# One exponential per head with both exponents as its bias, in the decay step of a bidirectional DeltaNet encoder

## The chip, the cores and the metric

The kernel runs on one core of one Trainium2 chip. The metric is the device time of one execution in microseconds (us), lower being better. The engines are TensorE (PE in the rows; its weight loads are PEld), VectorE (DVE), ScalarE (ACT), GpSimd (POOL) and SyncE (SP), whose queue issues all DMAs. Each engine works through its own list of instructions in a fixed order and waits there on semaphores.

## The reference

One encoder layer for two sequences, 4096 and 2048 rows of 1024, cut into 48 tiles of 128 rows. A combined projection feeds three groups of heads: windowed attention, attention to 256 memory rows, and a gated DeltaNet that runs over the sequence in both directions. The groups are gated, concatenated, projected and normalized. The change lies in the DeltaNet, in the decays:

```python
g = jnp.cumsum(g, axis=-1)
causal = jnp.tril(jnp.ones((C, C), bool))
decay = jnp.exp(jnp.where(causal, g[..., :, None] - g[..., None, :], -jnp.inf))
k_beta = k * beta[..., None]
a = jnp.einsum('...id,...jd->...ij', k_beta, k) * decay
...
qk = jnp.einsum('...id,...jd->...ij', q, k) * decay
```

The kernel holds these matrices transposed, the index j in the partitions. It puts the factor beta (and a constant scale, 2 to the power -20) into the same exponent. For one tile, direction and head an entry is exp(g_i + mask - g_j + ln beta_j - 20 ln 2), where g_i lies along the free axis and the last terms are one number per partition. The kernel takes chunks of 128 rows, one tile, instead of 64.

## The kernel before, in words

A first phase (lines 1503 to 1526) goes over 24 pairs of tiles: layer norm, projections, a short convolution and windowed attention; its results go to HBM. At its end stand `gates` for the first 8 tiles, the first call of `dn_front`, and the first gate projections (lines 1613 to 1616). A second phase (`pipe`, line 1724) goes over the 24 pairs twice, forwards and then backwards, as the DeltaNet runs. Beside the recurrence the forward pass does the gate projections and the memory attention (`gate_mem`, line 1686), the backward pass the output projection and the last layer norm (`finish`, line 1767).

What one tile and direction of the DeltaNet needs:

- `gates` (line 1362), once for 8 tiles, 6 calls in all: from the raw projections it computes ln beta (tile `lnb`, line 1387) and, by small matmuls into the PSUM tile `psg`, the cumulated g. ACT copies the transposed sums to `cT`, which goes to HBM as `crow`, and copies -g_j from PSUM to `ncum` (line 1410). A DVE instruction then adds LN20 and `lnb` into `psg` in place (line 1411), and ACT takes the exponential of all of it into `egs`.
- `dn_front` (line 1459), for two pairs together: it loads rows of `crow` into the tile `cr` (4 heads of 128x128 for one tile, called `e` in `dn_prep`) and calls `dn_prep`.
- `dn_prep` (line 869), 96 calls: DVE adds the mask to `cr` (line 882); ACT adds `ncum`, one instruction per head (line 884); ACT takes the exponential with `lnb` as bias, one per head (line 886). PE makes the products `psk`, and DVE multiplies them by `cr` into `n` and `p` (lines 898 and 899).
- `dn_invert` (line 933): `n` goes through HBM into `na`, POOL works 60 short instructions on `nb` and `tb`, and the result comes back as `uc`.
- `dn_level` and `dn_chain` (lines 983 and 1035): the recurrence over tiles. Each tile is a series of small matmuls (`psr`, `psx`, `psb`, `psx2`, `pss`); after each, ACT writes the rounded half of a result (`rx`, `shl`) and DVE the rest. DVE's `sf<-pss` ends a tile's link of the series.

The order of every engine's list comes from a planner (class `Plan`, line 56). It records all operations of a phase with a cost for each (`full_cost`, line 137) and schedules them by rank and by free buffers. Seven times it takes new ranks from how late each operation may be, and of the seven orders it keeps the one with the shortest planned span (`order`, line 268). An operation that goes or changes its engine can therefore move any other of its phase. All operations are issued at line 505, so the rows of the profile show that line, and are told apart by tile names.

```python
for h in range(4):
    S.activation(e[:, h], e[:, h], AF.Identity, bias=nc_[:, h:h + 1])
for h in range(4):
    S.activation(e[:, h], e[:, h], AF.Exp, bias=lb[:, h:h + 1])
```

Of the kernel before, what the change touches and what calls it, by code (L numbers as in the profile page):

```python
# [13 lines left out]
AF = mybir.ActivationFunctionType  # L14
ALU = mybir.AluOpType
# [535 lines left out]
def encoder(ctx: ExitStack, tc: tile.TileContext, A, outs):  # L551
    nc = tc.nc
    plan = Plan(tc)
    V, S, G, T, Q = plan.engines()
# [12 lines left out]
    def ctile(shape, dt, name):  # L567
        return const.tile(shape, dt, name=name, tag=name)
# [219 lines left out]
    ncum = ctile([P, 2, NT, 4], F32, "ncum")  # L788
    lnb = ctile([P, 2, NT, 4], F32, "lnb")
# [18 lines left out]
    def split(eng_hi, dst_h, dst_l, src, scale=None):  # L808

        if scale is None:  # L810
            S.activation(dst_h, src, AF.Copy)
            V.tensor_tensor(dst_l, src, dst_h, op=ALU.subtract)
        else:
            S.activation(dst_h, src, AF.Copy, scale=scale)
            V.scalar_tensor_tensor(dst_l, src, scale, dst_h, op0=ALU.mult, op1=ALU.subtract)
# [53 lines left out]
    def dn_prep(pool, psp, dr, t, e, n):  # L869

        fm = pool.tile([P, 8, P], F16, tag="fm", name="fm", bufs=2)
        Q.dma_start_transpose(out=fm, in_=dst_d[t].rearrange("p h t s d -> p (h t s d)"))

        ks = pool.tile([P, 4, P], F16, tag="ks", name="ks", bufs=KSB)
        kv = fm.rearrange("p (h t) m -> p h t m", t=2)[:, :, 1]
        for i in range(2):
            S.activation(ks[64 - 64 * i:128 - 64 * i], kv[64 * i:64 * i + 64], AF.Copy)
        lb = lnb[:, dr, t]
        nc_ = ncum[:, dr, t]
        d = {}  # L880

        V.tensor_tensor(e, e, dmask[dr][2].unsqueeze(1).to_broadcast([P, 4, P]), op=ALU.add)
        for h in range(4):
            S.activation(e[:, h], e[:, h], AF.Identity, bias=nc_[:, h:h + 1])
        for h in range(4):
            S.activation(e[:, h], e[:, h], AF.Exp, bias=lb[:, h:h + 1])
        d["eg"] = egs[:, :, dr, t]

        p = pool.tile([P, 4, P], F32, tag="p", name="p", bufs=1)
        for hp in range(2):  # L890
            hs = slice(2 * hp, 2 * hp + 2)
            psk = psp.tile([P, 2, 2, P], F32, tag="fr", name="psk", bufs=1)
            for h2 in range(2):
                h = 2 * hp + h2
                T.matmul(psk[:, :, h2], lhsT=fm[:, 2 * h + 1, :], rhs=fm[:, 2 * h:2 * h + 2, :],
                         start=True, stop=False)
                T.matmul(psk[:, :, h2], lhsT=ks[:, h, :], rhs=fm[:, 2 * h:2 * h + 2, :], start=False, stop=True)
            V.tensor_tensor(n[:, hs], psk[:, 1], e[:, hs], op=ALU.mult)
            V.scalar_tensor_tensor(p[:, hs], psk[:, 0], -(2.0 ** 10), e[:, hs], op0=ALU.mult, op1=ALU.mult)
        d["n"] = n  # L900
        phl = pool.tile([P, 2, 4, P], F16, tag="phl", name="phl", bufs=2 * PAIRS)
        split(None, phl[:, 0], phl[:, 1], p)
        d["phl"] = phl
        d["t"], d["dr"] = t, dr
        return d
# [247 lines left out]
    bias = biasp.tile([P, AH, 386], F32, name="bias", tag="bias")  # L1153
# [208 lines left out]
    def gates(b, pool, tags):  # L1362

        ts = slice(b * NG, min(NT, b * NG + NG))
        n = ts.stop - ts.start
        xe = pool.tile([P, 2, NG, 16], F32, tag=tags[0][0], name="gx", bufs=tags[0][1])
        w = pool.tile([P, 6, NG, 16], F32, tag=tags[1][0], name="gw", bufs=tags[1][1])[:, :, 0:n]
        x, e = xe[:, 0, 0:n], xe[:, 1, 0:n]
        Q.dma_start(out=x, in_=ab_d[b])
        z = w[:, 0]  # L1370
        V.tensor_tensor(z[:, :, 0:8], x[:, :, 0:8], dtb.unsqueeze(1).to_broadcast([P, n, 8]), op=ALU.add)
        V.tensor_scalar(z[:, :, 8:16], x[:, :, 8:16], -1.0, None, op0=ALU.mult)

        V.tensor_scalar(w[:, 1], z, -1.0, None, op0=ALU.mult)
        V.tensor_tensor(e, z, w[:, 1], op=ALU.min)
        S.activation(e, e, AF.Exp)
        V.tensor_scalar(w[:, 2], e, 2.0, None, op0=ALU.add)
        V.reciprocal(w[:, 2], w[:, 2])
        V.tensor_tensor(w[:, 3], e, w[:, 2], op=ALU.mult)
        V.tensor_tensor(w[:, 4], w[:, 3], w[:, 3], op=ALU.mult)  # L1380
        V.tensor_scalar(w[:, 5], w[:, 4], 1.0 / 15.0, None, op0=ALU.mult)
        for k in range(6, 0, -1):
            V.scalar_tensor_tensor(w[:, 5], w[:, 5], 1.0 / (2 * k + 1), w[:, 4], op0=ALU.add, op1=ALU.mult)
        V.scalar_tensor_tensor(w[:, 5], w[:, 5], 1.0, w[:, 3], op0=ALU.add, op1=ALU.mult)
        V.tensor_scalar(z, z, 0.0, None, op0=ALU.max)
        V.scalar_tensor_tensor(z, w[:, 5], 2.0, z, op0=ALU.mult, op1=ALU.add)
        V.tensor_scalar(lnb[:, :, ts], z[:, :, 8:16].rearrange("p t (d h) -> p d t h", d=2), -1.0, -LN20,
                        op0=ALU.mult, op1=ALU.add)
        g = z[:, :, 0:8]
        V.tensor_tensor(g, g, nea.unsqueeze(1).to_broadcast([P, n, 8]), op=ALU.mult)  # L1390
        V.tensor_scalar(g, g, GMIN, None, op0=ALU.max)
        gg = xe[:, 1].rearrange("p t c -> p (t c)").bitcast(F16)[:, 0:16 * n]
        gg = gg.rearrange("p (a d t h) -> p a d t h", a=2, d=2, h=4)
        gd = g.rearrange("p t (d h) -> p d t h", d=2)
        V.tensor_copy(gg[:, 0], gd)
        V.tensor_tensor(gg[:, 1], gd, gg[:, 0], op=ALU.subtract)
        ps = pj.tile([P, 512], F32, tag="pw", name="psg", bufs=1)
        ps3 = ps[:, 0:24 * n].rearrange("p (i d t h) -> p i d t h", i=3, d=2, h=4)
        pst = ps[0:4 * n, 256:512].rearrange("p (d i) -> p d i", d=2)
        for dr in range(2):  # L1400
            U, L, _ = dmask[dr]
            for i, st in enumerate((U, L, ones16)):
                for a in range(2):
                    T.matmul(ps3[:, i, dr], lhsT=st, rhs=gg[:, a, dr], start=(a == 0), stop=(a == 1))
            for a in range(2):
                T.matmul(pst[:, dr], lhsT=gg[:, a, dr], rhs=U, start=(a == 0), stop=(a == 1))
        cT = pool.tile([P, 2, P], F32, tag=tags[2][0], name="cT", bufs=tags[2][1])[0:4 * n]
        S.activation(cT, pst, AF.Copy)
        Q.dma_start(out=crow_d[b].rearrange("d t h i -> (t h) d i"), in_=cT)
        S.activation(ncum[:, :, ts], ps3[:, 0], AF.Copy, scale=-1.0)  # L1410
        V.scalar_tensor_tensor(ps3[:, 1], ps3[:, 1], LN20, lnb[:, :, ts], op0=ALU.add, op1=ALU.add)
        S.activation(egs[:, :, :, ts], ps3, AF.Exp)

# [45 lines left out]
    def dn_front(pools, psp, dr, pairs, step=2):  # L1459

        H = 4 // len(pairs)
        ds, ns = [], []
        for pool, tiles in zip(pools, pairs):
            t0 = min(tiles)
            rows = []
            for t in range(t0, t0 + 2, step):
                cr = pool.tile([P, step, 4, P], F32, tag="cr", name="cr", bufs=2)
                Q.dma_start(out=cr.rearrange("p t h i -> p (t h i)"),
                            in_=crow_d[t // NG][dr, t % NG:t % NG + step].rearrange("t h i -> (t h i)").partition_broadcast(P))
                rows += [cr[:, i] for i in range(step)]  # L1470
            n = pool.tile([P, 2, 4, P], F32, tag="n", name="n", bufs=PAIRS)
            ns.append(n)
            ds.append([dn_prep(pool, psp, dr, t, rows[t - t0], n[:, i]) for i, t in enumerate(tiles)])
        for pool, ucs, two in zip(pools, dn_invert(pools, dr, ns, H), ds):
            for i, d in enumerate(two):
                d["uc"] = ucs[:, 4 * i:4 * i + 4]
        return ds
# [356 lines left out]
```

## Time and profile before

| what | value |
|---|---|
| median of 3 runs (lowest to highest) | 3352.14 us (3349.26 to 3354.52) |
| profiled execution | 3363.07 us |
| its span, first to last instruction | 3361.0 us |
| busy: PE, DVE, ACT, POOL | 2870.1, 2920.9, 2441.2, 1711.0 us |
| mean granted TensorE clock, share of full | 0.944 |

Busy time is the time in which an engine executes at least one of its instructions. The profile names for each idle stretch the event that ended it, and follows one chain of work back from the last instruction: at each step to what released it, or to the instruction ahead of it on its engine. The chain adds up to the span. Matmuls are pipelined, so a busy PE isn't at its peak.

### The profile page before, as it was taken

To read this page: it belongs to the slowest core of one execution; us is meant where nothing else is said; L and a number is where in the kernel's file an instruction comes from. 1 tells how busy PE (TensorE), PEld (TensorE's weight loads), DVE (VectorE), ACT (ScalarE), POOL (GpSimd) and SP (SyncE) were. 2 spreads that over 40 slices of the span, in tenths; PEclk is the share of its full clock that TensorE was granted. 3 is DMA by queue.
4 is the path that set the end of the run, shared out by engine and by line. 5 is a ranking of instruction groups with operands and counts; after the bars stand their busy time and mean duration, and the time that the engine had idled before them with its cause. 6 is when DMAs were issued, how large, how long until landed. Compare 5 with 4: busy or idle time off the path is not lost.

```text
span 3361.0 us, 82755 instructions
## 1 busy us (share of the span) xinstructions
PE 2870.1 (85%) x29856; PEld 1893.3 (56%) x29856; DVE 2920.9 (87%) x6850; ACT 2441.2 (73%) x6253; POOL 1711.0 (51%) x2611
## 2 busy tenths in 40 slices
PE   5788888788898887767899999999988988998988
PEld 4566666666676665444556555555554544444544
DVE  7999868799999989678889888888878988888997
ACT  4577656767777776688888878777877777777764
POOL 3644424344444334546645455455528666657662
PEclk9899998899999998878999999999998999999999
DMA  6999999999999999898678887778788777877775
GB/s 203 239 224 220 219 222 222 234 230 220 212 233 220 200 224 247 210 223 180 165 191 194 206 181 178 172 161 181 172 190 194 191 183 179 193 179 188 183 175 154
DMA packets 1336916, 671.43 MB, mean 200 GB/s; under 512 B 1127728, under 2 KB 1243312, under 8 KB 1332280
## 3 DMA queue, kind: packets, MB, share of 16 engines
q1 hardware_dynamic: 1336504, 666.14, 86.3%
q8 instruction: 234, 3.83, 0.5%
q14 instruction: 178, 1.46, 0.1%
HBM read 240.12 MB, written 181.49 MB: 125 GB/s over the span
## 4 chain that ended last, share of the span: by engine, by line
DVE 31%; PE 20%; POOL 15%; DMA 13%; issue 10%; ACT 8%; SPq 3%; POOLq 0%; ACTq 0%; DVEq 0%
POOL nb L505 5%; DVE acc L505 5%; POOL tb L505 5%; PE pso L505 5%; PE psg L505 5%; PE psf L505 3%; SPq L505 3%; DVE lg L505 3%; DVE aphl L505 3%; PE psk L505 2%; ACT lg L505 1%; PE psq L505 1%; DMA uc<-ud 1%; PE pslg L505 1%; DVE rx L505 1%
## 5 line engine op out<-in xcount | busy, mean ns | idle before, releaser
L505 PEld LDWEIGHTS <-xT 128*128 128x128 f16 x5760 | 535.5, 99 | 385.2 <-issue 52.5
L505 PE MATMUL psg<-w2a,xT 128*128 128x512 f16 (+1 forms) x2304 | 446.0, 334 | 9.6 <-DVE qtm L505 8.0
L505 PE MATMUL psf<-xT,w1f 128*128 128x256 f16 (+1 forms) x3600 | 439.9, 276 | 14.7 <-DMA xT<-xhl 6.3
L505 PEld LDWEIGHTS <-w1f 128*128 128x128 f16 x3600 | 341.7, 101 | 59.4 <-issue 10.8
L505 POOL TENSOR_TENSOR nb<-nb,tb 128x30 f32<-128x30 f32 (+6 forms) x750 | 348.6, 465 | 49.3
L505 POOL TENSOR_TENSOR tb<-nb,na 128x30 f32<-128x30 f32 (+6 forms) x750 | 342.6, 457 | 48.3
L505 ACT ACTIVATE lg<-lg,mx,scal 128x385 f32<-128x385 f32 (+1 forms) x384 | 263.8, 688 | 122.3 <-DVE mx L505 107.6
L505 PE MATMUL pslg<-kfm,qfm 128*128 128x128 f16 x2240 | 201.0, 233 | 164.1 <-DVE mx L505 149.4
L505 DVE SCALAR_TENSOR_TENSOR acc<-cb,cw,acc 128x256 f32<-128x256 f32 x576 | 329.8, 605 | 4.1 <-POOL cb L505 1.7
L505 PEld LDWEIGHTS <-qfm 128*128 128x128 f16 x2624 | 204.2, 104 | 222.3 <-issue 188.0
L505 PEld LDWEIGHTS <-yT 128*128 128x128 f16 x2304 | 200.1, 99 | 216.1 <-issue 27.7
L505 PE MATMUL pso<-w2a,yT 128*128 128x512 f16 x1152 | 311.4, 394 | 9.6 <-DMA yT<-yhl 7.1
L505 PE MATMUL pso<-w2b,yT 128*128 128x512 f16 x1152 | 298.9, 383 | 0.0
L505 PE MATMUL psg<-w2b,xT 128*128 128x512 f16 x1152 | 289.3, 382 | 3.8 <-DMA w2b<-w_d 3.8
L505 PE MATMUL psq<-w1t,xT 128*128 128x512 f16 x1152 | 287.0, 385 | 0.2 <-ACT cb L505 0.2
L505 DVE TENSOR_TENSOR aphl<-lg,aphl 128x768 f16<-128x768 f32 (+1 forms) x192 | 209.9, 1096 | 49.7 <-ACT aphl L505 49.3
L505 POOL TENSOR_TENSOR n<-raw 128x256 f32<-128x256 f16 x96 | 82.3, 867 | 262.2 <-DMA raw<-cfh 62.1
L505 DVE CUSTOM_DVE_ANT_0 lg<-pslg,bias 128x385 f32<-128x385 f32 (+1 forms) x384 | 195.3, 539 | 17.7 <-PE pslg L505 13.5
L505 POOL TENSOR_TENSOR x<-x,grow 128x1024 f32<-128x1024 f32 x52 | 128.0, 2462 | 121.8 <-ACT x L505 117.6
L505 PEld LDWEIGHTS <-th 64*64 64x64 f16 x2304 | 99.1, 111 | 131.1 <-issue 106.1
L505 PE MATMUL psk<-w1t,xT 128*128 128x272 f16 x1152 | 161.4, 287 | 13.5 <-DVE qktm L505 10.0
L505 PE MATMUL psx<-rx,th 64*64 64x64 f16 x2304 | 126.8, 197 | 41.3 <-DVE rx L505 29.8
(1026 smaller groups left out, 7607.8 us busy)
## 6 DMA issues: line engine op xcount, KB each, us to landing
x<-x SPq DMA_DIRECT2D x48, 512.0 KB, 4.3
xT<-xT SPq DMA_DIRECT2D x24, 1024.0 KB, 5.5
xT<-xT SPq DMA_DIRECT2D x48, 512.0 KB, 4.5
n<-dn SPq DMA_DIRECT2D x96, 256.0 KB, 3.3
r<-x SPq DMA_DIRECT2D x48, 512.0 KB, 4.4
out_dram<-r SPq DMA_DIRECT2D x48, 512.0 KB, 3.8
cr<-crow SPq DMA_DIRECT2D x47, 512.0 KB, 5.1
yhl<-yhl SPq DMA_DIRECT2D x48, 384.0 KB, 3.4
```

The costliest lines, as they stand in the source:

```text
L505: getattr(self.eng[o["e"]], o["name"])(*o["args"], **o["kw"])
```

## The change

The two bias terms are added once per 8 tiles, and one exponential per head takes the sum as its bias. `ncum` now holds -g_j + ln beta_j - 20 ln 2; it is written by DVE instead of ACT, still from `psg`, before `psg` is changed in place.

```diff
@@ dn_prep
-        lb = lnb[:, dr, t]
         nc_ = ncum[:, dr, t]
...
         for h in range(4):
-            S.activation(e[:, h], e[:, h], AF.Identity, bias=nc_[:, h:h + 1])
-        for h in range(4):
-            S.activation(e[:, h], e[:, h], AF.Exp, bias=lb[:, h:h + 1])
+            S.activation(e[:, h], e[:, h], AF.Exp, bias=nc_[:, h:h + 1])
@@ gates
-        S.activation(ncum[:, :, ts], ps3[:, 0], AF.Copy, scale=-1.0)
+        V.scalar_tensor_tensor(ncum[:, :, ts], ps3[:, 0], -1.0, lnb[:, :, ts], op0=ALU.mult, op1=ALU.add)
         V.scalar_tensor_tensor(ps3[:, 1], ps3[:, 1], LN20, lnb[:, :, ts], op0=ALU.add, op1=ALU.add)
```

The planner makes new orders from it for all engines. Three places show what moves. The first is ACT at the first call of `dn_front`, near the end of the first phase (`cr` is the decay tile; `lg`, `aphl` belong to the attention, `cfh` and `acc` to the convolution). Before:

```order
L505 ACTIVATE lg,mx<-lg,mx,scal 128x385 x4
L505 ACTIVATE cr<-cr,ncum 128x128 x2
L505 ACTIVATE cr<-cr,lnb 128x128 x2
L505 ACTIVATE cr<-cr,ncum 128x128 x2
L505 ACTIVATE cr<-cr,lnb 128x128 x2
L505 ACTIVATE cfh<-acc 128x512
L505 ACTIVATE cr<-cr,ncum 128x128
L505 ACTIVATE aphl<-lg 128x768
L505 ACTIVATE cr<-cr,ncum 128x128
L505 ACTIVATE cr<-cr,lnb 128x128 x2
```

Now:

```order
L505 ACTIVATE lg,mx<-lg,mx,scal 128x385 x4
L505 ACTIVATE cr<-cr,ncum 128x128 x7
L505 ACTIVATE cfh<-acc 128x512
L505 ACTIVATE cr<-cr,ncum 128x128
L505 ACTIVATE aphl<-lg 128x768
```

The additions are gone, and the exponentials of two tiles, now named with `ncum`, stand nearly in one piece. In all, ACT's list has 384 instructions `cr<-cr,ncum` and 384 `cr<-cr,lnb` before, and 384 and none now; the 6 copies to `ncum` are gone from it too.

The second is DVE in the first call of `gates` (`gx` is the input of the matmuls into `psg`, `qktm` belongs to the attention). Before:

```order
L505 TENSOR_TENSOR gx<-gw,gx 128x64
L505 SCALAR_TENSOR_TENSOR qktm<-psk_2841,qktm 128x128 x2
L505 SCALAR_TENSOR_TENSOR qktm<-psq,qktm 128x8x64
L505 SCALAR_TENSOR_TENSOR psg<-psg,lnb 128x64
L505 ISA lg,mx<-pslg_590,bias 128x385
```

Now:

```order
L505 TENSOR_TENSOR gx<-gw,gx 128x64
L505 SCALAR_TENSOR_TENSOR qktm<-psk_2841,qktm 128x128 x2
L505 SCALAR_TENSOR_TENSOR qktm<-psq,qktm 128x8x64
L505 SCALAR_TENSOR_TENSOR ncum<-psg,lnb 128x2x32
L505 SCALAR_TENSOR_TENSOR psg<-psg,lnb 128x64
L505 ISA lg,mx<-pslg_590,bias 128x385
```

The new instruction stands right ahead of the one that it must precede.

The third is DVE early in the forward pass, from the end of the recurrence's second tile, `sf<-pss`, to `rx`, with which the third tile goes on (`gate`, `qtm` and `mmx` belong to the gate projections and the memory attention). Before:

```order
L505 SCALAR_TENSOR_TENSOR sf<-pss,st__21316 128x256
L505 TENSOR_TENSOR b_21232<-n,b_21230 64x4x32
L505 TENSOR_TENSOR kc<-kc_21355,kc 128x512
L505 TENSOR_TENSOR shl<-sf,shl 128x256
L505 SCALAR_TENSOR_TENSOR v_21343<-psr,v_21343 128x256
L505 TENSOR_TENSOR phl<-p,phl 128x512
L505 SCALAR_TENSOR_TENSOR rx<-v_21343,rx 128x256
```

Now, with `rx` next after the last row:

```order
L505 SCALAR_TENSOR_TENSOR sf<-pss,st__21308 128x256
L505 TENSOR_TENSOR yhl<-gate,yhl 128x256
L505 TENSOR_TENSOR b_21224<-n,b_21222 64x4x32
L505 SCALAR_TENSOR_TENSOR p<-psk,cr 128x256
L505 TENSOR_TENSOR shl<-sf,shl 128x256
L505 SCALAR_TENSOR_TENSOR qtm<-psg_21516,qtm 128x4x64
L505 TENSOR_REDUCE mmx<-psml 128x2 x2
L505 TENSOR_SCALAR mmx<-mmx,scal 128x2 x2
L505 SCALAR_TENSOR_TENSOR v_21335<-psr,v_21335 128x256
L505 TENSOR_REDUCE wmxwo_d_21225<-psw 128x1
L505 TENSOR_TENSOR kc<-kc_21347,kc 128x512
L505 SCALAR_TENSOR_TENSOR gate<-oa,scal,gate 128x512
```

More work of the gate projections and the memory attention now stands between two links of the recurrence here. On PE, when the third to seventh tile of the recurrence reach `psb`, between 70 and 95 more matmuls into `psg` stand ahead of it than before; by the eighteenth tile the two orders have the same number ahead, within 12 of it from there to the thirtieth.

## Rows read from the trace of the kernel before

**Rows 1.** Engine totals of the page: busy us, share of the span, instructions.
```profile
PE 2870.1 (85%) x29856; PEld 1893.3 (56%) x29856; DVE 2920.9 (87%) x6850; ACT 2441.2 (73%) x6253; POOL 1711.0 (51%) x2611
```

**Rows 2.** The chain that ended last, shares of the span by engine.
```profile
DVE 31%; PE 20%; POOL 15%; DMA 13%; issue 10%; ACT 8%; SPq 3%; POOLq 0%; ACTq 0%; DVEq 0%
```

**Rows 3.** Busy time by stretch: start:end, length, busy us and instructions per engine, clock, DMA.
```profile
core 0: us, PE busy (x) PEld busy (x) DVE busy (x) ACT busy (x) POOL busy (x), PEclk, DMA share, GB/s
0.00:1430.00 1430.00, 1158.88 (x12256) 888.68 (x12256) 1250.69 (x2878) 967.99 (x2292) 620.97 (x542) 0.93 0.98 222
1430.00:1600.00 170.00, 125.92 (x1331) 78.72 (x1331) 139.17 (x352) 140.88 (x383) 89.97 (x187) 0.80 0.89 201
1600.00:2440.00 840.00, 772.26 (x8398) 482.76 (x8396) 730.33 (x1741) 669.78 (x1820) 447.59 (x886) 0.98 0.78 179
2440.00:3361.00 921.00, 813.00 (x7876) 443.14 (x7873) 800.68 (x1881) 662.51 (x1762) 552.50 (x998) 0.95 0.77 183
```

**Rows 4.** The same stretches for ACT instructions that touch `ncum`: length, busy, count.
```profile
0.00:1430.00 1430.00, 3.03 (x9) 0.93 0.98 222
1430.00:1600.00 170.00, 19.30 (x55) 0.80 0.89 201
1600.00:2440.00 840.00, 57.94 (x166) 0.98 0.78 179
2440.00:3361.00 921.00, 56.79 (x160) 0.95 0.77 183
```

**Rows 5.** Instruction durations, count: shortest/median/longest ns, first and last start.
```profile
L505 ACT ACTIVATE cr<-cr,ncum x384: 384/387/409, 1360.9 to 3204.1; 128x128 f32<-128x128 f32 x192
L505 ACT ACTIVATE cr<-cr,lnb x384: 384/387/407, 1361.5 to 3204.7; 128x128 f32<-128x128 f32 x192
L505 ACT ACTIVATE ncum<-psg x6: 197/197/198, 1346.6 to 2145.2; 128x64 f32<-128x64 f32 x6
L505 DVE SCALAR_TENSOR_TENSOR psg<-psg,lnb x6: 224/230/233, 1346.8 to 2145.8; 128x64 f32<-128x64 f32 x6
```

**Rows 6.** Order of time: start, us from first start to last end, engine, operation.
```profile
1706.96 1.27 ACT L505 ACTIVATE cr<-cr,ncum 128x128 f32<-128x128 f32 x4
...
1709.35 2.55 PE L505 MATMUL psg<-w2a,xT 128*128 128x512 f16 x11
```

**Rows 7.** Pieces of the chain on ACT's `cr`: start, us, how many; 39 pieces in all.
```profile
1360.85 1.29 ACT cr L505 x4
...
1523.90 2.04 ACT cr L505 x7
...
2105.22 2.92 ACT cr L505 x10
...
3203.29 0.40 ACT cr L505
```

**Rows 8.** Waits for ACT from 1480 us on: us in total, times, longest.
```profile
DVE rx L505 <- ACT rx L505: 27.1, 27, 5.2
...
PE psr L505 <- ACT shl L505: 19.6, 16, 3.0
```

**Rows 9.** From issue to landing of the loads of `cr`.
```profile
DMA to landing us min/median/max: 3.8/5.1/7.6
```

**Rows 10.** Busy time in slices of 84 us, columns as in rows 3.
```profile
336.00:420.00 84.00, 67.70 (x752) 52.14 (x750) 75.18 (x166) 56.45 (x138) 36.32 (x25) 0.94 1.00 220
420.00:504.00 84.00, 70.99 (x818) 58.22 (x816) 57.61 (x138) 49.25 (x121) 24.35 (x22) 0.94 1.02 222
...
2352.00:2436.00 84.00, 77.25 (x838) 48.19 (x837) 71.38 (x173) 69.13 (x192) 49.45 (x118) 0.98 0.77 173
2436.00:2520.00 84.00, 72.45 (x656) 44.42 (x654) 59.48 (x146) 60.67 (x160) 23.71 (x55) 0.95 0.87 189
```

**Rows 11.** Two links of the recurrence that follow each other, in order of time.
```profile
1546.86 0.38 DVE L505 SCALAR_TENSOR_TENSOR sf<-pss,st__21368 128x256 f32<-128x256 f32 x1
1559.28 0.41 DVE L505 SCALAR_TENSOR_TENSOR sf<-pss,st__21384 128x256 f32<-128x256 f32 x1
```

## The prediction

> **What bounds the kernel now.** Read the engine totals first. DVE is busy for 87% of the span, PE for 85%, ACT for 73% [rows 1]: the engine that the change relieves is third. The chain of work that ended last says the same more sharply. DVE holds 31% of it, PE 20%, POOL 15%, transfers 13%, and ACT 8%, which is about 269 us of 3361 [rows 2]. No engine is full and none holds even a third of the chain, so the end is set by a series that passes from engine to engine.
>
> Next cut the span where the work changes [rows 3]. Until 1430 us the first phase runs, until 2440 us roughly the forward pass with the gate projections, and then the backward pass with the output projection. In these long stretches ACT is behind DVE and PE. Between 1430 and 1600 us it is not: there ACT is busy for 140.88 of 170 us, DVE for 139.17 and PE for 125.92, at a mean granted clock of only 0.80, a mixture of its two levels (2.4 GHz is 1.0, 1.2 GHz is 0.5). That is the lead-in of the second phase, when decays are prepared for several tiles at once. If a saving on ACT counts in full anywhere, it counts there.
>
> Last look at the instructions themselves. 384 additions `cr<-cr,ncum` last 387 ns each [rows 5], but four of them in a row take 1.27 us from the first start to the last end [rows 6]. So each one holds ACT for (1.27 - 0.387) / 3 = 0.294 us, and the rest of its duration overlaps its neighbour. Of the 390 instructions that touch `ncum`, 55 lie in the lead-in, 166 in the rest of the forward stretch, 160 in the backward stretch, and 9 before [rows 4].
>
> **The removed additions.** ACT loses 384 x 0.294 = 112.9 us of work, 4.6% of its busy time. How much of that lies on the path? The chain names ACT's `cr` in 39 pieces, 24.05 us in all [rows 7]. The pieces don't tell additions from exponentials; these are equal in number and I halve: 12.0 us. Added up over the pieces of each stretch, the chain's `cr` is 1.29 us before 1430, 7.19 us in the lead-in, 10.97 us until 2440 and 4.60 us behind, so the halves are 0.65, 3.6, 5.5 and 2.3 us. Outside the lead-in I take the halves, 8.4 us: the other additions lie beside DVE and PE work, and their cover stays, since DVE and PE keep all of theirs.
>
> In the lead-in the saving is bounded by nothing below and by 55 x 0.294 = 16.2 us above, the case in which ACT alone sets the pace of these 170 us. The nearest row is the chain with 3.6 us; but ACT is the busiest engine there, so that work behind the additions also comes up. I take 5.6 us, nearer to the chain than to the upper bound. The sum over the stretches is 8.4 + 5.6 = 14.0 us.
>
> Could it be far more? From 1480 us on, the longest waits for ACT are DVE's for `rx`, 27.1 us, and PE's for `shl`, 19.6 us [rows 8]. These are waits for the rounded halves in the recurrence, and most of each is the duration of an ACT instruction that stays. So a gain of the whole 112.9 us is excluded.
>
> **The new instruction on DVE.** Six copies leave ACT, 197 ns each, 1.2 us in all. Six instructions with an added PSUM operand come to DVE; the nearest is its neighbour `psg<-psg,lnb` of the same size at 230 ns [rows 5], which gives 6 x 0.23 = 1.4 us. The bounds are nothing and 1.4 us; I take nothing. In the order it stands right ahead of `psg<-psg,lnb`, and both wait for the same matmuls, so DVE's queue stops no longer than before; what is queued behind, the logits of the attention at the first call, comes 0.23 us later. The exponentials now wait for DVE's `ncum` alone, and `cr` itself lands 5.1 us after its load is issued [rows 9], behind the transfer of `crow`. That covers 0.23 us many times. Without this cover each of the 6 calls would cost 0.23 us, the same 1.4 us.
>
> **The dependence that goes.** Each exponential had to wait for the addition on its own head. In the order before, the planner filled that gap by alternating two additions with two exponentials; now eight stand in a row. The gap was filled, so I price it at nothing. The masks, `psk` and the multiplications by `cr` stay. Where a decay was late, the next to be late is `psk` with `ks`, or the load of `cr`.
>
> **The new order.** Nearly every row of every engine's list moves, SP's and POOL's too, and the first phase moves although it loses only 8 additions. I forecast nothing for that and bound it by holes in the trace. Between 420 and 504 us DVE is busy for 57.61 us, against 75.18 us in the slice ahead: a hole of 17.6 us. At the turn from forward to backward it is busy for 59.48 us, against 71.38: 11.9 us [rows 10]. A new order may close such holes or open another.
>
> **The sum.** The profiled execution took 3363.07 us, 2.1 us more than its span and 10.9 us (0.3%) more than the median of the runs, 3352.14 us. Taking 14.0 us off it gives 3349.1; taken off the median, it gives 3338.1, so I predict **3338 us**, 0.4% less than before.
>
> **Rival 1: nothing comes of it.** The additions are on the chain only as the last of several that were nearly as late, and another takes over each time. For it: ACT's chain share of 8%, and that the 921 us of the backward stretch have only 4.60 us of `cr` on the chain. Against it: the lead-in, where ACT is the busiest engine. Time: between 0 and 6.7 us gained, say 3352 us. The Trainium skill has a rule that says so for the kernel as a whole: the page Perfetto Trace Analysis, section Identifying the Most-Contended Engine, says that the engine with the highest occupancy is the most contended one and should be optimized first. By that rule only the lead-in's additions would pay, and the sum would be at most 16.2 us, or none if the whole kernel is taken as one, since DVE leads [rows 1]. The trace agrees in part: DVE leads in chain and occupancy, but the chain passes over ACT too.
>
> **Rival 2: the new order delays the recurrence, and it comes out slower.** Place: the first tiles of the forward pass. There PE's list now has up to 95 more matmuls into `psg` ahead of the third to seventh tile, and DVE's list more of the same projections between `sf` and `rx`. Eleven such matmuls take 2.55 us [rows 6], or (2.55 - 0.38) / 10 = 0.217 us each with 0.38 us for the last one's own length; 95 cost 20.6 us. In the order before, links of the recurrence follow each other at 12.4 us there [rows 11]. If that is about the shortest they can, the delay isn't made up later, although the later tiles have less to wait for. Against it: PE is idle for 44 of the 170 us, so the matmuls may fill holes, and the clock of 0.80 could rise. It decides if more than 15 us of the 20.6 fall on the recurrence, for then 8.4 us gained elsewhere leave over 6.7 us lost. At the full price the time is 3352.1 - 8.4 + 20.6 = 3364 us. A new hole of 17.6 us elsewhere, with nothing gained, gives 3370 us.
>
> **A rival that the orders exclude:** that the additions stay in another form. ACT's list has 384 fewer instructions on `cr`, and no list has others for them.
>
> **How the numbers follow.** A measurement of this kernel can tell about 0.2% from no change, 6.7 us: faster means below 3345.4 us, slower above 3358.8 us. My forecast, with the larger gains of a full lead-in or a closed hole, gets 0.56. Rival 1, and a gain that a hole of the new order takes back, gets 0.21. Rival 2 and its like elsewhere get 0.23, since the orders change everywhere and only 14 us stand against that. The low end is the upper bound in the lead-in (10.6 us more) with both holes closed (29.5 us): 3338 - 40 = 3298, rounded to 3300. The high end is nothing gained and one hole opened, 3370, rounded up to 3371. The forecast's own range is 3310 to 3345 us.
>
> **What would show it.** In the changed kernel ACT's busy time should fall by 100 to 115 us, to about 2335 us, and DVE's stay within 15 us. The chain's `cr` on ACT should fall to some 12 us. In the lead-in ACT should stand behind DVE, and the forward stretch should end earlier by 10 us, the backward stretch take 2 us less. The first phase should last as long as before; if it differs by over 10 us, the order did that and not the additions. The prediction is wrong if the recurrence's third to seventh `sf` come later, counted from the start of the second phase, and stay late; or if the time moves by over 20 us with the same chain shares.

## The result, and the profile after

The changed kernel takes 3368.58 us (median of 4 runs, 3363.30 to 3371.20) against 3350.70 us for the kernel before in the same comparison. The ratio is 1.0052, with a 95% interval of 1.0034 to 1.0070: slower, by about 17 us. The forecast was 3338 us and faster. The time lies inside the range, near its high end, and the sign is wrong.

The engine totals of the changed kernel's page, as [rows 1]:

```profile
PE 2883.5 (86%) x29856; PEld 1908.2 (57%) x29856; DVE 2917.4 (87%) x6856; ACT 2335.5 (69%) x5863; POOL 1710.9 (51%) x2611
```

The change does what it says. ACT's busy time fell from 2441.2 to 2335.5 us, its instructions by 390; DVE gained 6 instructions. The instructions that touch `ncum`, as [rows 5]:

```profile
L505 ACT ACTIVATE cr<-cr,ncum x384: 384/387/408, 1378.3 to 3204.8; 128x128 f32<-128x128 f32 x192
L505 DVE SCALAR_TENSOR_TENSOR ncum<-psg,lnb x6: 211/224/225, 1367.3 to 2152.7; 128x64 f32<-128x64 f32 x6
```

The exponentials last 387 ns as before, the new instruction on DVE 224 ns. But the first exponential starts at 1378.3 us; in the profile before the first addition started at 1360.9 [rows 5]. So the kernel is already late where its first decay is made, and only 8 additions lie ahead of the second phase. Busy time by stretch, columns and bounds as in [rows 3], in the changed kernel:

```profile
0.00:1430.00 1430.00, 1159.22 (x12093) 890.56 (x12094) 1242.67 (x2847) 954.57 (x2247) 613.06 (x522) 0.91 0.98 221
1430.00:1600.00 170.00, 138.77 (x1340) 86.58 (x1340) 137.89 (x351) 128.72 (x337) 92.27 (x186) 0.86 0.88 199
1600.00:2440.00 840.00, 768.39 (x8424) 483.52 (x8419) 727.60 (x1755) 629.96 (x1661) 451.14 (x882) 0.97 0.80 181
2440.00:3361.00 921.00, 817.09 (x8007) 447.49 (x8006) 806.67 (x1904) 622.20 (x1620) 552.94 (x1022) 0.97 0.78 184
```

Read the counts. By 1430 us PE has issued 163 matmuls fewer than before and DVE 31 instructions fewer: the first phase is behind. In the lead-in ACT now stands behind DVE, as forecast, but that did not end the kernel earlier. The chain of waits on this page reaches only the last stretch of the run (its shares add up to about 3% of the span), so it can't be set beside [rows 2].

One thing about the profile before must be known. Its execution was 10.9 us above its median, so the two profiled executions differ by only 6.4 us of span where the medians differ by 18. A second profiled execution of the kernel before (the run `e_before2` below) has a span of 3342.4 us. From here on that one is "before", unless the first is named. It took 3344.42 us, some 5 us less than the median of the kernel before in its comparison (3348.97 us), so distances from it look larger by that much. One execution of the run `e_oldorder` below took 8617.89 us at a mean granted clock of 0.292 and is left out of that run's ratio.

### The profile page after: what moved, and what is told of

Its sections match the earlier page's. It is cut to its first block, busy times and chain, and to the rows that moved or that the text cites. A ratio compares the mean times of both kernels' runs of the same rounds, so it can differ in the third digit from the quotient of the medians.

```text
span 3367.4 us, 82337 instructions
## 1 busy us (share of the span) xinstructions
PE 2883.5 (86%) x29856; PEld 1908.2 (57%) x29856; DVE 2917.4 (87%) x6856; ACT 2335.5 (69%) x5863; POOL 1710.9 (51%) x2611
## 5 line engine op out<-in xcount | busy, mean ns | idle before, releaser
L505 PE MATMUL psk<-w1t,xT 128*128 128x272 f16 x1152 | 169.8, 296 | 19.8 <-DVE qktm L505 9.1
L505 PE MATMUL psov<-vtm,apt 128*128 128x64 f16 x3360 | 141.6, 199 | 28.1 <-DMA apt<-aphl 28.1
```

The source lines that it names most:

```text
L505: getattr(self.eng[o["e"]], o["name"])(*o["args"], **o["kw"])
```

## The experiments

The planner decides the order of each phase by itself, so work and order can be taken apart. In most of the runs below the planner is shown one set of operations, and another is issued in its place: an operation may carry a list of what it stands for. Each ratio is to executions of the kernel before in the same comparison. The diffs below are written out for each run; the runs' kernels hold all the variants and choose by a switch.

```diff
@@ class Plan, where the operations are issued
-                    getattr(self.eng[o["e"]], o["name"])(*o["args"], **o["kw"])
+                    for e, nm, args, kw in o.get("emit", [(o["e"], o["name"], o["args"], o["kw"])]):
+                        getattr(self.eng[e], nm)(*args, **kw)
```

**The additions gone, the order before in both phases.** The planner sees additions and exponentials; the additions issue nothing, the exponentials take the summed bias, and `ncum` is written by DVE.

```diff
@@ dn_prep, against the kernel before
         for h in range(4):
             S.activation(e[:, h], e[:, h], AF.Identity, bias=nc_[:, h:h + 1])
+            plan.ops[-1]["emit"] = []
         for h in range(4):
             S.activation(e[:, h], e[:, h], AF.Exp, bias=lb[:, h:h + 1])
+            plan.ops[-1]["emit"] = [("ACT", "activation", (e[:, h], e[:, h], AF.Exp), dict(bias=nc_[:, h:h + 1]))]
@@ gates
         S.activation(ncum[:, :, ts], ps3[:, 0], AF.Copy, scale=-1.0)
+        plan.ops[-1]["emit"] = [("DVE", "scalar_tensor_tensor", (ncum[:, :, ts], ps3[:, 0], -1.0, lnb[:, :, ts]),
+                                 dict(op0=ALU.mult, op1=ALU.add))]
```

> Both phases keep the order that the planner made for the kernel before; the additions are left out where they stood, and the new instruction stands where the copy to ncum stood. If the new order is what costs (my theory), this is faster than before by about the 14 us of the prediction: ratio 0.994 to 0.998. If the removed additions or the new bias cost by themselves (rival), it is slower, as the changed kernel is: 1.003 to 1.007. If the additions are worth nothing, 0.999 to 1.001.

Measured: 3349.81 us, ratio 1.0006 (0.9996 to 1.0017): neither my theory's gain nor the rival's loss, but the third case. The engine totals of its page:

```profile
PE 2868.8 (86%) x29856; PEld 1889.6 (56%) x29856; DVE 2923.1 (87%) x6856; ACT 2333.4 (70%) x5863; POOL 1706.1 (51%) x2611
```

ACT's busy time is that of the changed kernel, so the work is really gone, and apart from it the instructions of PE, DVE, ACT and POOL stand in the order before. In an unchanged order the whole saving is worth nothing that can be measured.

**The additions back, the new order in both phases.** The planner sees the changed operations; each exponential issues an addition and an exponential.

```diff
@@ dn_prep, against the changed kernel
         for h in range(4):
             S.activation(e[:, h], e[:, h], AF.Exp, bias=nc_[:, h:h + 1])
+            plan.ops[-1]["emit"] = [
+                ("ACT", "activation", (e[:, h], e[:, h], AF.Identity), dict(bias=nc_[:, h:h + 1])),
+                ("ACT", "activation", (e[:, h], e[:, h], AF.Exp), dict(bias=lb[:, h:h + 1]))]
@@ gates
         V.scalar_tensor_tensor(ncum[:, :, ts], ps3[:, 0], -1.0, lnb[:, :, ts], op0=ALU.mult, op1=ALU.add)
+        plan.ops[-1]["emit"] = [("ACT", "activation", (ncum[:, :, ts], ps3[:, 0], AF.Copy), dict(scale=-1.0))]
```

> Both phases in the order of the changed kernel, but with the additions put back, each right ahead of its exponential, and the copy to ncum back on ACT. If the new order costs: slower than the changed kernel, because ACT's 113 us come back into an order that has no room for them, ratio 1.007 to 1.015. If the removed additions cost by themselves: near the kernel before, 0.998 to 1.002.

Measured: 3410.23 us, ratio 1.0187 (1.0170 to 1.0204), above the range that I gave. With the additions back the new order is 1.9% slower than the order before; without them it is 0.5% slower. But this isn't the order alone. ACT is busy for 2482.0 us here and for 2442.2 us before, 39.8 us more with the same instructions, since each exponential now stands right behind the addition on its own head (start, us, engine, operation):

```profile
1526.40 0.40 ACT L506 ACTIVATE cr<-cr,ncum 128x128 f32<-128x128 f32 x1
1526.83 0.40 ACT L506 ACTIVATE cr<-cr,lnb 128x128 f32<-128x128 f32 x1
1527.13 0.39 ACT L506 ACTIVATE cr<-cr,ncum 128x128 f32<-128x128 f32 x1
```

The exponential starts 0.43 us after the addition that it needs, when that has ended; the next addition, on another head, starts 0.30 us after the exponential and overlaps it. So put back in this way the additions cost 1.0187 - 1.0052 = 1.35%, about 45 us, where in the order before they cost nothing. How much of it is the order's lack of room and how much this placing, isn't told apart. The four runs of the table below are free of it: ACT is busy in them for 2333.4 to 2335.5 us.

**One phase's order at a time, the additions gone.** The first of these two has the first phase in the order before and the second in the new one, the other the reverse. The only edit is which operations the planner is shown in which phase.

```diff
@@ dn_prep, against the first experiment; gates alike
-        for h in range(4):
-            S.activation(e[:, h], e[:, h], AF.Identity, bias=nc_[:, h:h + 1])
...
+        if PLANNED[0] == "two":
+            for h in range(4):
+                S.activation(e[:, h], e[:, h], AF.Identity, bias=nc_[:, h:h + 1])
...
+        else:
+            for h in range(4):
+                S.activation(e[:, h], e[:, h], AF.Exp, bias=nc_[:, h:h + 1])
@@ between the phases
     p1.close()
+    PLANNED.pop(0)
```

> The additions gone; the first phase in the old order, the second in the new one. The changed kernel's trace has the first result of the inversion (uc) arrive 18 us later than before, so theory one puts the cost into the first phase's order: ratio 0.995 to 1.001. If the second phase's order costs (the recurrence's tiles that the prediction's second rival names), 1.003 to 1.007.

Measured with the first phase in the order before: 3338.92 us, ratio 0.9971 (0.9956 to 0.9986).

> The additions gone; the first phase in the new order, the second in the old one. If the first phase's order costs: 1.001 to 1.005, the 18 us less what the missing additions give back. If the second phase's order costs: 0.994 to 0.999.

Measured with the second phase in the order before: 3369.15 us, ratio 1.0074 (1.0057 to 1.0091), above the 1.001 to 1.005 that I had expected.

These four make a table of ratios, all without the additions:

| | second phase: order before | second phase: new order |
|---|---|---|
| first phase: order before | 1.0006 | 0.9971 |
| first phase: new order | 1.0074 | 1.0052 |

The first phase's new order costs 0.0068 or 0.0081, about 23 to 27 us. The second phase's new order gives 0.0035 or 0.0022, about 12 to 7 us; the first difference is clear of the intervals, the second isn't. The traces tell the same of the first phase. The rows are the first copies of the inverted blocks on ACT, with which the second phase begins; before, then with the first phase in the order before, then the changed kernel, then with only the first phase's order new (name, count, ns, first and last start):

```profile
L505 ACT ACTIVATE tc__21287<-uc x1: 309/309/309, 1432.5 to 1432.5; 128x128 f16<-128x128 f32 x1
```
```profile
L506 ACT ACTIVATE tc__21279<-uc x1: 309/309/309, 1432.6 to 1432.6; 128x128 f16<-128x128 f32 x1
```
```profile
L505 ACT ACTIVATE tc__21279<-uc x1: 310/310/310, 1455.9 to 1455.9; 128x128 f16<-128x128 f32 x1
```
```profile
L506 ACT ACTIVATE tc__21279<-uc x1: 309/309/309, 1454.6 to 1454.6; 128x128 f16<-128x128 f32 x1
```

Both kernels with the new first phase are 22 to 24 us late there. Six profiled executions with the first phase in the order before, with or without its 8 additions, reach this point between 1430.2 and 1437.9 us, so in these six an execution alone moves it by less than 8 us. How far each stands from before at later points of the recurrence (start of a tile's `sf`, us):

| point | before | additions gone, order before | changed kernel | first phase in the order before | second phase in the order before |
|---|---|---|---|---|---|
| first `tc<-uc` | 1432.5 | +2.9 | +23.5 | +0.1 | +22.1 |
| first `sf` | 1489.1 | +3.1 | +14.0 | -10.8 | +22.7 |
| third | 1539.7 | +2.3 | +31.7 | +9.3 | +23.7 |
| seventh | 1595.2 | +1.7 | +29.7 | +10.0 | +24.8 |
| 25th | 1970.1 | -2.1 | +19.8 | -4.5 | +15.8 |
| 37th | 2206.9 | -3.5 | +18.2 | -8.9 | +15.6 |
| 49th | 2499.2 | +1.4 | +26.3 | -2.4 | +21.3 |
| 96th | 3333.8 | +4.4 | +25.0 | -13.2 | +23.4 |

In the changed kernel's column the whole loss is there when the second phase begins: 23.5 us, and 25.0 at the end.

**Where the first phase loses it.** DVE, the busiest engine, has the same work there in both kernels: until the first `tc<-uc` it is busy for 1252.88 us before and for 1255.08 us in the changed kernel. So the loss is idle time of DVE, 21 us more of it. About half has come by 1200 us, where DVE has worked 1057.26 us instead of 1067.78. Two stretches show it, one ahead of that point and one behind. Before:

```profile
480.00:720.00 240.00, 197.96 (x2187) 157.30 (x2186) 193.68 (x470) 161.96 (x386) 93.00 (x72) 0.91 1.04 230
...
1320.00:1380.00 60.00, 38.83 (x318) 23.05 (x315) 45.91 (x116) 32.38 (x83) 18.18 (x25) 0.86 1.04 293
```

And in the changed kernel:

```profile
480.00:720.00 240.00, 193.40 (x2110) 155.44 (x2111) 184.46 (x414) 154.00 (x362) 84.58 (x69) 0.88 1.04 231
...
1320.00:1380.00 60.00, 45.40 (x341) 29.17 (x339) 34.64 (x91) 25.86 (x63) 11.23 (x14) 0.91 0.93 271
```

In the first, DVE works 9.2 us less, and PE does 77 matmuls fewer at a mean granted clock of 0.88 instead of 0.91. DVE's longest wait there is 3.8 us, so this loss is spread over many waits; whether PE's lower clock adds to it or only follows from PE's own waits isn't shown. In the second, DVE works 11.3 us less. There a long wait is seen, a chain of idle engines in the changed kernel (start, us, engine, operation, idle time before it and what ended it, in order of time):

```profile
1328.16 0.79 SPq L505 DMA_DIRECT2D dn<-n  x1
...
1336.11 1.29 POOL L505 TENSOR_TENSOR n<-raw 128x256 f32<-128x256 f16 x2 [9.21 <-DMA dn<-n]
1337.43 0.63 ACT L505 ACTIVATE nsq<-n 128x512 f32<-128x512 f32 x1 [8.42 <-POOL n L505]
...
1338.10 0.69 DVE L505 TENSOR_REDUCE nss<-nsq 128x8 f32<-128x512 f32 x1 [8.09 <-ACT nsq L505]
...
1338.60 1.75 PE L505 MATMUL psk<-w1t,xT 128*128 128x272 f16 x7 [6.66 <-ACT cb L505]
```

POOL wants to write the next `n`, whose buffer is still being sent to HBM by a transfer issued at 1328.16 us. It lands after 7.8 us, where the median of the eight such transfers between 1200 and 1400 us is 2.8. ACT waits for POOL, DVE for ACT, PE for ACT: four engines stand for 6.7 to 9.2 us at the same time. With the new first phase and the second in the order before, the same row is there again (POOL 7.37 us, DVE's `nss` 5.9 us); in the run with the additions gone and the order before, DVE's longest wait there is 4.5 us, for other work. POOL's wait itself isn't new: in the kernel before it waits 5.53 us for that transfer, at 1320.67 us, but ACT stands only 0.49 us behind it. So one wait of some 8 us on DVE is seen that the order before hasn't. How much of the 23 us goes back to it isn't shown: the order before has waits of its own nearby, and a run that takes this one away wasn't tried. The rest isn't traced to single rows.

**Is the new first phase worse in itself, or a draw?** The next four runs plan the first phase once more, with one latency in the planner's table changed by 1 ns. The work is the changed kernel's, and so is the second phase's order.

```diff
@@ class Plan, for the first phase only
-    LAT = {"PE": 200.0, "DVE": 150.0, "ACT": 170.0, "POOL": 40.0, "SP": 0.0}
+    LAT = {"PE": 201.0, "DVE": 150.0, "ACT": 170.0, "POOL": 40.0, "SP": 0.0}
```

> The changed kernel with the same work and the same second phase; only the first phase is planned once more, with PE's latency in the planner's table at 201 ns instead of 200. So the first phase has another order of the same operations. Theory A (the order that the planner happens to find is a draw, and the change drew a bad one): the ratio to the kernel before falls anywhere from 0.992 to 1.010, and the three draws of this kind differ among each other by more than 0.003. Theory B (a first phase without the additions is planned worse in itself): the ratio stays within 0.002 of the changed kernel's 1.0052, in all three draws.

Measured: 3352.77 us, ratio 1.0013 (1.0000 to 1.0026).

The same edit with DVE at 151.0:

> The changed kernel with the same work and second phase, the first phase planned with DVE's latency at 151 ns instead of 150. Theory A (a draw): the ratio to before lies anywhere from 0.992 to 1.010, apart from the other draws by more than 0.003. Theory B (worse in itself): 1.003 to 1.007 again.

Measured: 3354.53 us, ratio 1.0019 (1.0007 to 1.0031).

The same with ACT at 171.0:

> The changed kernel with the same work and second phase, the first phase planned with ACT's latency at 171 ns instead of 170. Theory A (a draw): the ratio to before lies anywhere from 0.992 to 1.010, apart from the other draws by more than 0.003. Theory B (worse in itself): 1.003 to 1.007 again.

Measured: 3345.20 us, ratio 0.9996 (0.9983 to 1.0008).

And PE at 201.0, with the first phase planned from the operations before:

> As the run with the first phase in the order before, the second in the changed kernel's order and the additions gone (0.9971), but the first phase is planned with PE's latency at 201 ns, from the operations before. Theory A (a draw): the ratio moves off 0.9971 by more than 0.002, the order before having been a lucky one more likely than not, so to 0.999 to 1.008. Theory B (orders planned with the additions are good in themselves): 0.995 to 0.999.

Measured: 3359.67 us, ratio 1.0040 (1.0024 to 1.0055). Its plan sees the additions, and still it loses 0.7% against the order that the same operations had before.

None of the three draws from the changed operations repeats 1.0052, so theory B falls as it was put. They differ among each other by 0.0023, less than the 0.003 that I had asked of theory A, but with the changed kernel the four span 0.0056, and the two orders planned from the operations before, 0.9971 and 1.0040, span 0.0069. The order of the first phase is a draw of some 0.4% either way: tiny changes of the planner's inputs give other orders and other times. The changed kernel has the slowest of the six, with an interval that overlaps that of 1.0040. Whether orders planned without the additions are a little slower on the average, four of them against two can't tell.

The six traces say where it happens. From the lowest ratio to the highest (0.9971, 0.9996, 1.0013, 1.0019, 1.0040, 1.0052) the first `tc<-uc` starts at 1432.6, 1439.7, 1447.2, 1445.7, 1457.8 and 1455.9 us. The second phase has the same order in all six, and the time follows the start of it: 25 us there, 27 us by the ratios.

**Is the second phase a draw too?** The first phase in the order before, the additions gone, the second phase planned from the changed operations with ACT's latency at 171 ns, then with PE's at 201:

```diff
@@ between the phases, against the run with the first phase in the order before
     p1.close()
     PLANNED.pop(0)
+    Plan.LAT = {"PE": 200.0, "DVE": 150.0, "ACT": 171.0, "POOL": 40.0, "SP": 0.0}
```

> The first phase in the order before, the additions gone (as in the run that gave 0.9971), and the second phase planned from the changed operations with ACT's latency at 171 ns in the planner's table. Theory A (the second phase's order is as much a draw as the first's): off 0.9971 by more than 0.002, somewhere between 0.993 and 1.005. Theory B (the second phase without additions is planned better in itself): 0.995 to 0.999 again.

Measured: 3336.57 us, ratio 0.9951 (0.9934 to 0.9968), the fastest version here. It and the run at 0.9971 beat both kernels.

> The same with PE's latency at 201 ns for the second phase. Theory A (a draw): off 0.9971 by more than 0.002, somewhere between 0.993 and 1.005, and not equal to the other draw within 0.001. Theory B (planned better in itself): 0.995 to 0.999 again.

Measured: 3352.12 us, ratio 1.0004 (0.9992 to 1.0017). The two differ by 0.0053, which is theory A; the first of them alone lies within theory B's range. So planning without the additions doesn't assure a gain: one of the three orders has none. But all three lie at or below 1.0006, the one order that was planned with them, so a small gain on the average isn't excluded.

This run's page has a chain over the whole span, as [rows 2]:

```profile
DVE 29%; PE 23%; POOL 14%; DMA 13%; issue 10%; ACT 8%; SPq 3%; POOLq 0%; ACTq 0%; DVEq 0%
```

Its pieces on ACT's `cr`, as [rows 7] (start, us, how many), the ones in the lead-in and the longest one:

```profile
1530.14 0.29 ACT cr L506
...
1531.52 0.48 ACT cr L506 x2
...
1533.20 0.29 ACT cr L506
...
2358.87 1.75 ACT cr L506 x6
```

All 13 pieces add up to 6.9 us, where the profile before had 24.05. In the lead-in 1.06 us are left of 7.19. So 17 us of `cr` have left the chain, more than I forecast, and yet ACT still holds 8% of it and the time is that of before: other work has come up in its place. The second phase's order is a new one here too, so what left with the additions and what with the order isn't told apart; the chain of the run in the unchanged order reaches only the end of its span.

**Before, once more, and with more work on ACT.**

> The kernel before, once more, for a second profiled execution of it: the first one took 0.3% more than the median of its runs. Every theory expects a ratio of 1.000 within 0.002 and a span between 3335 and 3362 us. If the span is near 3348 us, it is to be set beside the run with the order before and without the additions (span 3346.8 us), stretch by stretch: theory A (the additions' time becomes idle time of ACT, and nothing else moves) expects each of the four stretches to end within 4 us of that run; theory B (they save some 5 us in the lead-in, which are lost again later) expects the third tile's sf at least 4 us later than in that run and the end level with it.

Measured: 3344.14 us, ratio 0.9991 (0.9976 to 1.0005), span 3342.4 us. It is set beside the run without additions in the table above. The ends of the stretches lie within 2.9, 1.7, 1.4 and 4.4 us of each other; the third tile's `sf` is 2.3 us earlier here, not later. That is theory A but for the last 0.4 us. One thing speaks for a small gain that is lost again: from the first `tc<-uc` to the 37th `sf` both executions of before take longer, 774.4 and 776.4 us, than the run without additions, 768.1 us. The 6 to 8 us saved there are not in the time at the end, by the interval of 1.0006. Where they are lost stays open: against one execution of before it is at the turn and behind it, against the other it is not seen.

The last run keeps the order before and adds work:

```diff
@@ dn_prep, against the kernel before
             S.activation(e[:, h], e[:, h], AF.Identity, bias=nc_[:, h:h + 1])
+            plan.ops[-1]["emit"] = [
+                ("ACT", "activation", (e[:, h], e[:, h], AF.Copy), {}),
+                ("ACT", "activation", (e[:, h], e[:, h], AF.Identity), dict(bias=nc_[:, h:h + 1]))]
```

> The kernel before, its order kept on every engine, but with one more pass of ACT over each head of cr right ahead of the addition, a copy in place: 384 more ACT instructions, 112.9 us of work by the durations of the additions, the values unchanged. Theory A (the order was planned with room for just the ACT work that it had, so taking work out gains nothing and putting work in costs): slower by 0.5 to 1.5%, a ratio of 1.005 to 1.015. Theory B (ACT has slack beside the chain in both directions): within 0.3% of before. Theory C (my first sum, 14.0 us for 112.9 us, holds in both directions): a ratio of 1.003 to 1.006.

Measured: 3373.03 us, ratio 1.0076 (1.0056 to 1.0095), about 25 us. Its engine totals:

```profile
PE 2879.9 (85%) x29856; PEld 1892.9 (56%) x29856; DVE 2921.7 (87%) x6850; ACT 2552.5 (76%) x6637; POOL 1709.3 (51%) x2611
```

ACT is busy for 110.3 us more than before (2442.2). The ratio is in theory A's range. Its interval touches the upper end of theory C's, but C wanted a gain from the removal as well, and the first experiment has none. So in one and the same order, about 110 us of ACT work taken out give nothing, and 110 us put in cost 25. The copy also lengthens the series of instructions on each head, and whether that costs or ACT's time isn't told apart.

## Why the prediction was wrong

**The new order: this step failed.** The prediction said "I forecast nothing for that", and bounded it by two holes of 17.6 and 11.9 us [rows 10]. The order alone, with the work held fixed, came to 1.0052 - 1.0006 = 0.0046, about 15 us slower, made of 23 to 27 us lost in the first phase and 7 to 12 us gained in the second. The first phase went beyond the bound: a hole in one trace says how much could be closed there, not how much a new order can lose in small pieces over 1430 us. The wider hole, between 420 and 504 us, was even narrowed in the changed kernel, where DVE works 65.35 us in that slice against 58.52 before, and the phase came out late all the same. With the 2 us of the next paragraph these 15 make the 17 us.

**The removed additions: mis-sized.** 14.0 us were summed; the unchanged order gives 1.0006, that is 2 us slower, with an interval from 1.3 us faster to 5.7 us slower. The amount of work was right (112.9 us forecast, 108.8 measured as ACT's busy time in the order before). The step from chain to time was wrong: half of the chain's `cr` counted as gained, as though nothing stood close behind it, and 0.4% were forecast on that. The lead-in was taken at 5.6 us and up to 16.2; counted from the first `tc<-uc`, the seventh `sf` comes 1.2 us earlier there. In the forward stretch as a whole 6 to 8 us showed, against 5.5 + 5.6 forecast, and they were not there at the end.

**Rival 1** (nothing comes of it) was right for the work by itself. Its mechanism, that others take over on the chain, is seen only in the run above whose second phase has a new order too. The rule beside it, in the Trainium skill's page Perfetto Trace Analysis, section Identifying the Most-Contended Engine, is that the engine with the highest occupancy should be optimized first. The runs agree with it for work that is removed, ACT being third with 73%. They set a limit to its use: the same engine was no slack to be filled, as the added 110 us cost 0.76%.

**Rival 2** (the recurrence's third to seventh tile delayed) happened, and wasn't the cause. With the first phase in the order before and the second in the new one, the first `sf` comes 10.8 us earlier and the third 9.3 us later than before; so the first to third tile take 20.1 us longer, against the 20.6 that I had priced. The matmuls are there: between these two starts PE issues 192 matmuls into `psg` and is busy with them for 42.10 us, before 108 for 26.59 us. That is 15.5 us of the 20.1; that the whole agrees with the price to half a microsecond is luck. The rows of the two, before and then this run (name, count, ns, first and last start):

```profile
L505 DVE SCALAR_TENSOR_TENSOR sf<-pss,st__21300 x1: 411/411/411, 1489.1 to 1489.1; 128x256 f32<-128x256 f32 x1
...
L505 DVE SCALAR_TENSOR_TENSOR sf<-pss,st__21368 x1: 385/385/385, 1539.7 to 1539.7; 128x256 f32<-128x256 f32 x1
```
```profile
L506 DVE SCALAR_TENSOR_TENSOR sf<-pss,st__21292 x1: 411/411/411, 1478.2 to 1478.2; 128x256 f32<-128x256 f32 x1
...
L506 DVE SCALAR_TENSOR_TENSOR sf<-pss,st__21360 x1: 408/408/408, 1549.0 to 1549.0; 128x256 f32<-128x256 f32 x1
```

The changed kernel shows the same, 17.7 us. But the delay doesn't stay: by the 25th tile it is gone, and the last `sf` is 13.2 us earlier. The argument that links of 12.4 us [rows 11] couldn't make it up was wrong, since the later tiles don't follow at that pace: from the 7th to the 25th, before takes 374.9 us, or 20.8 us a tile, and the new order 360.4. "Its like elsewhere" was what came.

**Right:** ACT's busy time (2335.5 us, about 2335 forecast), DVE's within 15 us (3.5 less), 224 ns for the new instruction against 230 and no wait of an exponential for it, and ACT behind DVE in the lead-in. That the alternation of additions and exponentials filled a gap was right as well, as the run with the additions back shows (0.43 us from start to start without it, 0.30 with another head between). The order now has seven exponentials in a row and the eighth behind `cfh`, not eight, and nothing hangs on that. The mark set ahead also worked: "if it differs by over 10 us, the order did that and not the additions". It differed by 18 us between the two profiles that were at hand, by 23 against the second one. Not so the two stretches: from the first `tc<-uc` to the 49th `sf` the changed kernel takes 2.8 us more where 10 us less were forecast, and from there to the last `sf` 1.3 us less, against 2.

**The chances.** 0.23 for slower was too little. The traces gave a change of order everywhere against a saving of 14 us. The draws measured here, six for the first phase and four for the second, range over 0.8% and 0.55% of the time; a saving of 0.4% doesn't outweigh such a draw, and one of nothing leaves the sign to it.

## What to carry to other kernels

Where a planner orders the work, an edit is two changes: the work, and a new order that owes it little. Measure them apart by issuing the new work in the old order, and draw several orders by tiny changes of the planner's inputs before the edit is judged; here the best of a few draws gave 0.5%, the edit in its old order nothing. An engine's share of the chain need not be a saving, since other work can stand just behind it, and removing and adding the same work on such an engine need not have opposite effects.

## What the runs showed of the hardware

An ACT copy in place without a bias is shorter than an addition of a bias to the same 128x128 tile: 293 against 402 ns, in the run with both (count, shortest/median/longest ns):

```profile
L506 ACT ACTIVATE cr<-cr x384: 292/293/312, 1360.2 to 3215.4; 128x128 f32<-128x128 f32 x192
L506 ACT ACTIVATE cr<-cr,ncum x384: 401/402/404, 1360.5 to 3215.8; 128x128 f32<-128x128 f32 x192
```

The exponential with a bias lasts 386 ns there, and the addition 387 in the kernel before [rows 5]. The Trainium skill's page ScalarE: Activation LUTs, section What ACT_TABLE_LOAD costs, states about 93 ns for each operand that is one number per partition: 293 + 93 is the exponential's 386, while the addition took 16 ns more.

The 16 ns don't belong to the addition: the second of two instructions in a row on the same head has them. With the additions back in the new order it is the exponential that stands second, and it lasts 401 ns and the addition 386:

```profile
L506 ACT ACTIVATE cr<-cr,ncum x384: 384/386/403, 1382.4 to 3245.9; 128x128 f32<-128x128 f32 x192
L506 ACT ACTIVATE cr<-cr,lnb x384: 401/401/404, 1382.8 to 3246.4; 128x128 f32<-128x128 f32 x192
```

There the second starts only after the first has ended (0.43 us from start to start), where neighbours on different heads overlap (0.30 us).

A kernel's own executions vary more than I had thought: in one comparison the 28 runs of the kernel before lie between 3336.84 and 3356.44 us, 0.6%. With 11 or 12 runs of a kernel against 21 to 28 of the one before, the intervals above reach 0.10 to 0.13% to either side, so that a difference of 0.2% is only just told.
